# Three unused pieces of storage between the tiles of a two-block transformer kernel

## The chip, the cores and the metric

The kernel runs on 1 core of one Trainium2 chip. The metric is device time in microseconds for one execution; of the kernel before, three runs gave 2788.84, 2790.34 and 2790.70 us, median 2790.34.

## The reference, cut to what matters

256 tokens of width 2048 go through two transformer blocks in float32. Each of their large steps is a product of a [256, 2048] activation with a weight matrix:

```python
x = first_block(x, mem, ...)      # input projection (5136 columns), causal pooling and gated delta rule,
                                  # output projection; cross attention on 256 memory rows; gated
                                  # convolution FFN of width 5632
return second_block(x, c_2, ...)  # modulation vectors from c; projection to NSA and MoBA attention;
                                  # output projection; squared-ReLU FFN of width 8192
# e.g.
h = modulate(rms_norm_2(x, pre_norm_ffn[l]), shift_f, scale_f)
f = jnp.square(jax.nn.relu(h @ w_up[l])) @ w_down[l]
x = x + gate_f[:, None, :] * rms_norm_2(f, post_norm_ffn[l])
```

## The kernel before, in words

**Split products.** Every large product is made of float32r matmuls: an operand is split into a high part and the rest (low part), and high x high, high x low and low x high are summed in PSUM. So each block of a product takes three matmuls, a triple.

**Weights.** `load_to` (L193) brings a unit of 128 x 1024 weights into one of four `w32` buffers by a DMA from SP's queue. `split_to` (L207) makes its high part `wh` on ScalarE (L216) and its low part `wl` on VectorE (L218), three buffers each. The units run in one planned order through the whole program, loaded seven ahead and split two or three ahead.

**Activations.** They lie transposed, features on partitions, in eight tiles A0 to A7 of 8192 bytes per partition, each holding 8 feature blocks of 256 tokens. `act_pair(0)` (L412) is A0, A1 for the high parts and A2, A3 for the low parts; `act_pair(1)` is A4, A5 and A6, A7. The hidden rows of both feed-forward networks and the second block's attention outputs use `hidden` (L1258) with A4 and A6 or A5 and A7, high part first.

**The two loops.** `lin_a` (L285) gives rows of tokens: an activation block of 128 x 128 is stationary and 512 weight columns move (L298, L299, L300). `lin_b` (L304) gives transposed results: a weight block of 128 x 128 is stationary and 256 tokens of an activation block move (L316, L317, L318). In both, the second weight part is read with the activations' high part, and the activations' low part with the high weights:

```python
mm(ps, h, wh[:, k, :], start=kb == 0, stop=False)          # L298, lin_a: stationary first, then moving
mm(ps, h, wl[:, k, :], start=False, stop=False)            # L299
mm(ps, lo, wh[:, k, :], start=False, stop=kb == g.nkb - 1) # L300
mm(ps, wb, h, start=..., stop=False, ...)                  # L316, lin_b
mm(ps, wb, lo, start=False, stop=False, ...)               # L317
mm(ps, wb2, h, start=False, stop=kb == g.nkb - 1, ...)     # L318
```

**Who reads which tiles.** lin_b reads A0 to A3 in the input projection, the queries of the cross attention, gate and up of the first FFN, the second block's projections and its up products; it reads A4 to A7 only for the memory keys (`mk`, L653). lin_a reads A0 to A3 for z, the mixer output and the second block's values; it reads A4 to A7 for the memory values, both attention outputs and the down products of both FFNs.

**Order.** The program records its instructions itself, in the order of the code: after each weight unit `pump` steps the pending tasks (evacuations, norms, attention, the modulation's sums), so that their instructions stand between the matmuls.

**Addresses.** Tiles get their place in the order in which their tags first occur, one after the other, and the weights' buffers follow. By the built program (start in bytes of a partition, modulo 256 and modulo 512):

| tiles | before, mod 256 | after, mod 256 | before, mod 512 | after, mod 512 |
|---|---|---|---|---|
| A0 to A3 | 192 | 128 | 192 | 384 |
| A4, A5 | 0 | 192 | 256 | 448 |
| A6, A7 | 128 | 192 | 384 | 192 |
| wh, wl, w32 (ten buffers) | 192 | 192 | 448 | 448 |
| cst, X, prm, r0 to r3 | 128 | 128 | | |
| most other r and s tiles | 64 | 128 | | |

Blocks within A tiles are 1024 bytes apart, blocks of 128 columns or tokens 512 bytes, so a tile's phase modulo 512 is that of every block that a matmul reads in it.

Of the kernel before, what the change touches and what calls it, by code (L numbers as in the profile page):

```python
# [9 lines left out]
F32 = mybir.dt.float32  # L10
# [5 lines left out]
P = 128  # L16
# [74 lines left out]
class Prog:  # L91
# [21 lines left out]

# [1 line left out]
    def t(self, tag, shape, dt=F32):  # L115
        self.seq += 1
        return self.pool.tile(shape, dt, tag=tag, name=f"{tag}_{self.seq}")

    def col(self, name, n):
# [18 lines left out]

# [1 line left out]
    def start(self, gen, rate=1.0):  # L140
# [21 lines left out]
    def need(self, *tasks):  # L162
        """Steps these tasks to their ends, and the others only where these wait for something."""
        n = 0
        while any(not t["done"] for t in tasks):
            n += 1
            assert n < 10000, "tasks wait for each other"
            self.blocked = False
            for task in tasks:
                self.step(task)  # L170
            if self.blocked:
                for task in list(self.tasks):
                    if task not in tasks and task["rate"] >= 1.0:
                        self.step(task)
# [11 lines left out]

# [1 line left out]
    def plan(self, groups):  # L188
# [42 lines left out]

# [1 line left out]
    def group_start(self):  # L233
# [13 lines left out]
    def lin_small(self, name, n, xh, xl, tag):  # L247
        """[256, 2048] x [2048, n] of few columns in one bank; returns it, with the low parts' products beside."""
        nc = self.nc
# [71 lines left out]

# [1 line left out]
    def c(self, name):  # L323
# [17 lines left out]
    def rms_cols(self, name, parts):  # L341
        """parts [P, 2, n] of partial sums of squares over D -> [P, 2] 1/rms."""
        nc = self.nc
        s = self.col(name + "_s", 2)
        r = self.col(name, 2)
        nc.vector.tensor_reduce(s, parts, axis=AX, op=OP.add)
        self.powm(r, s, 1.0 / D)
        return r

    def row_bcast(self, colv, name, pause=0):  # L350
        """[P, 2] columns -> [P, 256], the same row in every partition."""
        nc = self.nc
        dg = self.t("dd", [P, 2, P])
        for tb, eng in enumerate((nc.gpsimd, nc.vector)):
            eng.tensor_scalar(dg[:, tb], self.c("ident"), colv[:, tb:tb + 1], 1.0, op0=OP.mult, op1=OP.mult)
        yield from self.pause(pause)
        tag, ps = yield from self.get_bank()
        for tb in range(2):
            nc.tensor.matmul(ps[:, tb * P:(tb + 1) * P], self.c("ones"), dg[:, tb], start=True, stop=True)
        row = self.t(name, [P, T])  # L360
        nc.scalar.activation(row, ps[:, :T], AF.Copy)
        self.give(tag)
        return row
# [12 lines left out]
    def lift(self, src, kb0, gcol, dst, nb=4):  # L376
        """Transposes token rows of nb feature blocks, times a column per block, as high and low parts."""
        nc = self.nc
# [17 lines left out]
    def lift_t(self, src, kb0, gcol, dst, nb=4):  # L396
        """The same from rows that come transposed."""
        nc = self.nc
        hi, lo = dst
        for b in range(nb):  # L400
            kb = kb0 + b
            nc.scalar.activation(hi(kb), src[:, b], AF.Copy, scale=gcol(kb))  # L402
            nc.vector.scalar_tensor_tensor(lo(kb), src[:, b], gcol(kb), hi(kb).bitcast(F32),
                                           op0=OP.mult, op1=OP.subtract)
            if b % 2:
                yield
# [5 lines left out]
    def act_pair(self, half):  # L412
        """High and low parts of [2048, 256] in one half of the activations' space."""
        a = [self.t(f"A{4 * half + j}", [P, 8, T], F32R) for j in range(4)]

        def part(o):
            return lambda kb, n=0: a[o + kb // 8][:, kb % 8:kb % 8 + n] if n else a[o + kb // 8][:, kb % 8, :]

        return part(0), part(2)
# [29 lines left out]
    def lift_evac(self, accs, c, parts, gcol, dst):  # L449
        """Adds products to rows, with their squares' sums, and lifts the rows."""  # L450
        nc = self.nc
# [43 lines left out]

# [1 line left out]
    def run(self):  # L497
# [48 lines left out]

# [1 line left out]
        self.consts = {"cst": self.pool.tile([P, _CONST["cst"].shape[1]], F32, name="cst")}  # L548
# [15 lines left out]
        nc.gpsimd.memset(self.mhalf, -0.5)  # L564
        nc.scalar.activation(self.col("first", 8), self.mhalf, AF.Copy)

# [1 line left out]
        self.split_to(1)  # L568
# [38 lines left out]
        A4 = self.t("A4", [P, 2, 4, T])  # L607
        A5 = self.t("A5", [P, 2, 4, T])
        S = [{"k": A4[:, 0], "q": A4[:, 1], "v": A5[:, 0]}, {}]
        self.z = [None, None]  # L610
# [27 lines left out]

# [1 line left out]
        self.y = self.act_pair(0)  # L640
# [15 lines left out]

# [1 line left out]
        yh, yl = self.y  # L658
# [15 lines left out]

# [1 line left out]
        vm = []  # L676
# [11 lines left out]

# [1 line left out]
        oh, ol = self.act_pair(1)  # L690
# [32 lines left out]

# [1 line left out]
    def rr_evac(self, accs, dst, row):  # L725
# [75 lines left out]

# [1 line left out]
    def pool_evac(self, accs, c):  # L803
# [44 lines left out]

# [1 line left out]
    def mem_lift(self, c):  # L850
# [11 lines left out]

# [1 line left out]
    def bc(self, colv):  # L864
# [100 lines left out]
    def dn_batch(self, tb, hs, qT, knT, vb, kbe, kd, o, rq, st):  # L965
# [67 lines left out]
        def even(x, b):  # L1033
            """Columns of the even blocks of b."""
            return x.rearrange("p (n two b) -> p n two b", two=2, b=b)[:, :, 0]
# [56 lines left out]

# [1 line left out]
    def xattn(self, h, qT, kT, v, oh, ol):  # L1094
# [47 lines left out]
    def later_split(self, tag, psv, hi, lo):  # L1142
        """High and low parts of a bank, one step on."""
        def gen():
# [4 lines left out]

# [1 line left out]
    def ada(self, vectors, stage, acct, width):  # L1151
# [44 lines left out]
    def gain_rows(self, gcol, tags):  # L1196
        """[P, 16] columns -> [P, 2048], the same row in every partition."""
        nc = self.nc
# [22 lines left out]

# [1 line left out]
    def gate_evac(self, accs, c):  # L1223
# [67 lines left out]

# [1 line left out]
    def before_mixer2(self):  # L1293
# [29 lines left out]
    def last_evac(self, accs, c):  # L1323
        """Rows after the first block, the two norms' squares, and the rows transposed."""
        nc = self.nc
# [20 lines left out]
    def hold(self, c, take):  # L1346
        """Four transposed feature blocks of the rows in two banks."""
        nc = self.nc
# [11 lines left out]
    def spare_acc(self, pr):  # L1360
        """The accumulators that the group after the next one takes."""
        tag = f"acc{(self.acc_next + 2 + pr) % 4}"
# [4 lines left out]
    def unhold(self, c, G, held, vec=False, prs=(0, 1)):  # L1367
        """Those blocks times columns, in float32."""
        nc = self.nc
# [11 lines left out]
    def modulate(self, c, rr, shift, dst, G=None, held=None):  # L1381
        """Rows' scale and the shift on four blocks, as high and low parts."""
        nc = self.nc
# [135 lines left out]
    def gain_evac(self, accs, dst, c, parts, gr):  # L1519
        """Sums two slabs' products, their rows' squares, and the gains on them."""  # L1520
        nc = self.nc
# [126 lines left out]
    def probs(self, q, k, gate, ptag, stag, nm):  # L1648
        """Causal softmax rows of one head, times a gate, transposed: key block 0 for all 256 queries, then key
        block 1 for the later 128."""  # L1650
        nc = self.nc
# [46 lines left out]
    def nsa_cmp(self, g, qn):  # L1698
        """Gated softmax over the compressed keys, transposed, for four heads; two heads per tile."""
        nc = self.nc  # L1700
# [45 lines left out]
    def nsa_group(self, g, qn, ksw, vsw, oh, ol):  # L1746
        """Four heads; the next head's rows begin while a head's last steps run."""
        nc = self.nc
# [26 lines left out]
    def both(self, gens, apart=0):  # L1775
        """Steps generators side by side, each starting some steps after the one before."""
        out = [None] * len(gens)
# [36 lines left out]

# [1 line left out]
    def relu_evac(self, accs, c, hid):  # L1816
# [11 lines left out]
    def ffn2(self):  # L1828
# [3 lines left out]
        F = [None] * 4  # L1832
        fp = self.parts("f_p")
        hid = {}

# [50 lines left out]
def columns(inputs):  # L1886
    """Small vectors with features on partitions."""
    parts = []
# [43 lines left out]
```

## Time and profile before

| | |
|---|---|
| median of three runs | 2790.34 us (2788.84 to 2790.70) |
| span of the profiled execution | 2786.8 us, first to last instruction |
| TensorE matmul busy | 2736.6 us, 98% |
| TensorE weight load busy | 2514.3 us, 90% |
| VectorE / ScalarE / GpSimd busy | 66% / 47% / 10% |
| HBM traffic | 579.21 MB read, 209 GB/s over the span |

The page is of one execution; its whole time is not listed apart from the span, and the runs' times lie 2 to 4 us above that span. The durations of matmuls overlap: the next one starts while the one before still drains, so the sum of the durations is more than the busy time. The matmul's first named operand is the one that moves, the second is the stationary one.

### The profile page before, as it was taken

The numbers are of one execution on the slowest core, as the hardware profiler recorded it, in microseconds if no ns is written. First come the engines' busy times: TensorE is split into PE (matmuls) and PEld (weight loads), VectorE is DVE, ScalarE is ACT, GpSimd is POOL, SyncE is SP. The second block draws the span as 40 slices with busy tenths as digits, with TensorE's granted clock in tenths as the row PEclk, the third lists the DMA queues.
The fourth block names the chain that finished last, engine by engine and source line by source line (L and its number), as shares of the span: only waits on it lengthen the run. The fifth ranks groups of instructions, "written<-read, shape, count | busy, mean of one in ns | idle before, by whom it ended". The sixth has DMA issues, their size and how long they took to land.

```text
span 2786.8 us, 45609 instructions
## 1 busy us (share of the span) xinstructions
PE 2736.6 (98%) x18322; PEld 2514.3 (90%) x18322; DVE 1849.6 (66%) x2276; ACT 1299.8 (47%) x1894; POOL 290.9 (10%) x249
## 2 busy tenths in 40 slices
PE   8999999999999999999999989999989999999997
PEld 8999998889889999999999789998889988999896
DVE  6665745676787877777777576677575556655555
ACT  6544533544454454444444554444554444444443
POOL 0230201000001020000000031001021000000020
PEclk9999999999999999999999999999999999999999
DMA  8644544787787777777777645443556666656554
GB/s 290 190 129 136 175 129 144 233 292 249 235 265 267 261 256 258 271 260 255 271 257 241 211 149 179 144 144 129 181 167 229 233 219 233 224 184 185 187 181 143
DMA packets 292116, 584.29 MB, mean 210 GB/s; under 512 B 23968, under 2 KB 32288, under 8 KB 291904
## 3 DMA queue, kind: packets, MB, share of 16 engines
q1 hardware_dynamic: 287952, 569.93, 62.5%
q0 software_dynamic: 3232, 10.14, 1.1%
q8 instruction: 143, 2.34, 0.3%
q10 hardware_dynamic: 720, 1.31, 0.1%
q14 instruction: 69, 0.57, 0.1%
HBM read 579.21 MB, written 2.10 MB: 209 GB/s over the span
## 4 chain that ended last, share of the span: by engine, by line
PE 88%; issue 6%; DVE 2%; ACT 1%; POOL 1%; DMA 0%; DVEq 0%; ACTq 0%; POOLq 0%
PE acc L316 16%; PE acc L318 16%; PE acc L317 16%; PE acc L298 11%; PE acc L300 11%; PE acc L299 11%; DVE wl L218 1%; PE m L986 1%; PE m L1039 1%; ACT wh L216 1%; PE m L1046 1%; PE m L1136 0%; PE m L1105 0%; PE m L989 0%; PE m L1694 0%
## 5 line engine op out<-in xcount | busy, mean ns | idle before, releaser
L218 DVE TENSOR_TENSOR wl<-w,wh 128x1024 fp32r<-128x1024 f32 x874 | 1092.0, 1251 | 871.4 <-ACT wh L216 869.1
L216 ACT ACTIVATE wh<-w 128x1024 fp32r<-128x1024 f32 x880 | 928.2, 1058 | 1200.7 <-PE acc L317 652.7
L316 PE MATMUL acc<-A,wh 128*128 128x256 f32 x3968 | 1137.5, 287 | 11.3 <-ACT A L402 7.8
L318 PE MATMUL acc<-A,wl 128*128 128x256 f32 x3968 | 1126.2, 284 | 5.0 <-DVE wl L218 2.7
L317 PE MATMUL acc<-A,wh 128*128 128x256 f32 x3968 | 1125.9, 284 | 0.1
L316 PEld LDWEIGHTS acc<-A,wh 128*128 128x128 f32 x3968 | 761.9, 192 | 13.1 <-ACT A L402 7.8
L318 PEld LDWEIGHTS acc<-A,wl 128*128 128x128 f32 x3968 | 761.6, 192 | 5.6 <-DVE wl L218 2.9
L317 PEld LDWEIGHTS acc<-A,wh 128*128 128x128 f32 x3968 | 762.2, 192 | 2.0 <-DVE A L1400 0.5
L298 PE MATMUL acc<-wh,A 128*128 128x512 f32 x1536 | 612.5, 399 | 2.4 <-ACT wh L216 2.1
L300 PE MATMUL acc<-wh,A 128*128 128x512 f32 x1536 | 608.0, 396 | 0.0
L299 PE MATMUL acc<-wl,A 128*128 128x512 f32 x1536 | 602.9, 393 | 2.0 <-DVE wl L218 2.0
L299 PEld LDWEIGHTS acc<-wl,A 128*128 128x128 f32 x1536 | 288.6, 188 | 69.6 <-DVE wl L218 3.5
L300 PEld LDWEIGHTS acc<-wh,A 128*128 128x128 f32 x1536 | 288.6, 188 | 66.9
L298 PEld LDWEIGHTS acc<-wh,A 128*128 128x128 f32 x1536 | 289.5, 188 | 63.8 <-ACT wh L216 2.6
L1188 DVE SCALAR_TENSOR_TENSOR r<-r,c_silu_c,r 128x1024 f32<-128x1024 f32 x128 | 172.2, 1346 | 0.0
L1822 POOL TENSOR_TENSOR s<-s 128x512 f32<-128x512 f32 x32 | 51.0, 1592 | 574.1 <-ACT s L1821 574.1
L1188 DVE SCALAR_TENSOR_TENSOR s<-s,c_silu_c,s 128x512 f32<-128x512 f32 x128 | 95.8, 749 | 12.0 <-DMA s<-w_ada 10.6
L1243 POOL TENSOR_TENSOR r<-r,rr 128x1024 f32<-128x1024 f32 x11 | 26.8, 2434 | 590.2 <-ACT r L1242 546.4
L1666 ACT ACTIVATE s<-s,c_am 128x128 f32<-128x128 f32 (+1 forms) x48 | 21.5, 448 | 90.3 <-DVE c_am L1664 90.3
L1554 POOL TENSOR_TENSOR r<-r,s 128x512 f32<-128x512 f32 x15 | 25.6, 1706 | 227.8 <-DVE s L1551 227.8
L1239 DVE SCALAR_TENSOR_TENSOR r<-r,prm,r 128x254 f32<-128x254 f32 x88 | 42.3, 481 | 1.6
L374 ACT ACTIVATE dd<-X 128x512 bf16<-128x512 f32 x40 | 25.1, 628 | 23.5 <-DVE X L437 15.8
(368 smaller groups left out, 1636.4 us busy)
## 6 DMA issues: line engine op xcount, KB each, us to landing
w<-w_up SPq DMA_DIRECT2D x216, 512.0 KB, 3.7
w<-w_down SPq DMA_DIRECT2D x216, 512.0 KB, 3.8
w<-w_in SPq DMA_DIRECT2D x152, 512.0 KB, 3.5
r<-w_ada SPq DMA_DIRECT2D x128, 512.0 KB, 5.0
w<-w_gate SPq DMA_DIRECT2D x88, 512.0 KB, 3.9
w<-w_xkv SPq DMA_DIRECT2D x64, 512.0 KB, 3.9
s<-w_ada SPq DMA_DIRECT2D x128, 256.0 KB, 4.8
w<-w_mix_out SPq DMA_DIRECT2D x32, 512.0 KB, 3.6
```

What stands on the lines that cost most here:

```text
L216: nc.scalar.activation(hi[:, :m], src[:, :m], AF.Copy)
L218: eng.tensor_tensor(lo[:, :m], src[:, :m], hi[:, :m].bitcast(F32), op=OP.subtract)
L298: mm(ps, h, wh[:, k, :], start=kb == 0, stop=False)
L299: mm(ps, h, wl[:, k, :], start=False, stop=False)
L300: mm(ps, lo, wh[:, k, :], start=False, stop=kb == g.nkb - 1)
L316: mm(ps, wb, h, start=kb == 0 and b % 2 == 0, stop=False, skip_group_check=True)
L317: mm(ps, wb, lo, start=False, stop=False, skip_group_check=True)
L318: mm(ps, wb2, h, start=False, stop=kb == g.nkb - 1, skip_group_check=True)
L986: return lambda out, h: nc.tensor.matmul(out, lhs(h), rhs(h), start=True, stop=True)
L1188: nc.vector.scalar_tensor_tensor(acc, tiles.pop(n), self.silu_c[:, kb:kb + 1], acc, op0=OP.mult, op1=OP.add)
L1239: nc.vector.scalar_tensor_tensor(cv[:, b, s:], st[:, b, :T - s], w[k], cv[:, b, s:], op0=OP.mult, op1=OP.add)
L1822: nc.gpsimd.tensor_tensor(y, y, y, op=OP.mult)
```

## The change

A method `pad` allots a tile that nothing reads or writes. It is called three times: before A0's first use (48 float32, 192 bytes per partition), after A4 and A5 (128 bytes), and after most other tiles (192 bytes). Tiles that come later in the order move up by that much, so A0 to A5 by 192 bytes, A6, A7 and the scratch by 320 and the weights by 512. Comments and docstrings are taken out as well. The built program has the same instructions in the same order on every engine, with the same waits; only addresses and line numbers differ.

```diff
+    def pad(self, name, n):
+
+        return self.pool.tile([P, n], F32, tag=name, name=name)
...
         nc.scalar.activation(self.col("first", 8), self.mhalf, AF.Copy)
-
-        # ---- first block: input projection ----
+        self.pad("pad0", 48)
+
+
         self.split_to(1)
         xh, xl = self.act_pair(0)
...
         A4 = self.t("A4", [P, 2, 4, T])
         A5 = self.t("A5", [P, 2, 4, T])
+        self.pad("pad1", 32)
         S = [{"k": A4[:, 0], "q": A4[:, 1], "v": A5[:, 0]}, {}]
...
         fp = self.parts("f_p")
+        self.pad("pad2", 48)
         hid = {}
```

## Rows read from the trace of the kernel before

**Rows 1.** The page's head: busy time, share, instructions; granted clock in 40 slices.

```profile
PE 2736.6 (98%) x18322; PEld 2514.3 (90%) x18322; DVE 1849.6 (66%) x2276; ACT 1299.8 (47%) x1894; POOL 290.9 (10%) x249
PEclk9999999999999999999999999999999999999999
```

**Rows 2.** The chain that ended last, by engine.

```profile
PE 88%; issue 6%; DVE 2%; ACT 1%; POOL 1%; DMA 0%; DVEq 0%; ACTq 0%; POOLq 0%
```

**Rows 3.** Waits of PE, longest in total first: us, times, longest.

```profile
PE acc L316 <- ACT A L402: 7.8, 1, 7.8
PE m L1356 <- DVE X L1499: 4.4, 1, 4.4
PE acc L316 <- ACT A L1395: 3.5, 2, 1.7
...
```

**Rows 4.** The page's costliest groups: count, busy us, mean ns, idle before.

```profile
L316 PE MATMUL acc<-A,wh 128*128 128x256 f32 x3968 | 1137.5, 287 | 11.3 <-ACT A L402 7.8
...
L298 PE MATMUL acc<-wh,A 128*128 128x512 f32 x1536 | 612.5, 399 | 2.4 <-ACT wh L216 2.1
```

**Rows 5.** PE in order of time, second FFN, lin_b: start us, duration us.

```profile
2189.83 0.29 PE L316 MATMUL acc<-A,wh 128*128 128x256 f32 x1
...
2198.47 0.28 PE L316 MATMUL acc<-A,wh 128*128 128x256 f32 x1
```

**Rows 6.** Groups by line, PE, 2190 to 2220 us.

```profile
L316 PE MATMUL acc<-A,wh 128*128 128x256 f32 x84 | 23.8, 283 | 0.0
```

**Rows 7.** PE in order of time, memory keys, lin_b.

```profile
321.25 0.28 PE L317 MATMUL acc<-A,wh 128*128 128x256 f32 x1
...
329.38 0.28 PE L317 MATMUL acc<-A,wh 128*128 128x256 f32 x1
```

**Rows 8.** Groups by line, PE, 322 to 329 us.

```profile
L318 PE MATMUL acc<-A,wl 128*128 128x256 f32 x21 | 5.9, 282 | 0.0
L316 PE MATMUL acc<-A,wh 128*128 128x256 f32 x21 | 5.9, 281 | 0.0
L317 PE MATMUL acc<-A,wh 128*128 128x256 f32 x20 | 5.6, 279 | 0.0
```

**Rows 9.** PE in order of time, second FFN, lin_a.

```profile
2504.92 0.39 PE L298 MATMUL acc<-wh,A 128*128 128x512 f32 x1
...
2520.92 0.39 PE L298 MATMUL acc<-wh,A 128*128 128x512 f32 x1
```

**Rows 10.** Groups by line, PE, 2505 to 2540 us.

```profile
L300 PE MATMUL acc<-wh,A 128*128 128x512 f32 x51 | 20.2, 397 | 0.0
L298 PE MATMUL acc<-wh,A 128*128 128x512 f32 x51 | 20.0, 393 | 0.0
L299 PE MATMUL acc<-wl,A 128*128 128x512 f32 x51 | 20.0, 392 | 0.0
```

**Rows 11.** PE in order of time, mixer output, lin_a.

```profile
480.06 0.39 PE L298 MATMUL acc<-wh,A 128*128 128x512 f32 x1
...
495.70 0.39 PE L298 MATMUL acc<-wh,A 128*128 128x512 f32 x1
```

**Rows 12.** Groups by line, PE, 478 to 518 us.

```profile
L298 PE MATMUL acc<-wh,A 128*128 128x512 f32 x59 | 23.1, 391 | 0.0
L300 PE MATMUL acc<-wh,A 128*128 128x512 f32 x59 | 23.0, 389 | 0.0
L299 PE MATMUL acc<-wl,A 128*128 128x512 f32 x59 | 23.0, 389 | 0.0
```

**Rows 13.** Two lines of plain float32 matmuls: duration ns min/median/max, first and last start.

```profile
L1105 PE MATMUL m<-r,r x64: 377/379/380, 648.2 to 762.5; 128*128 128x256 f32 x64
L1136 PE MATMUL m<-s,r x64: 377/379/379, 669.3 to 783.1; 128*128 128x256 f32 x64
```

**Rows 14.** One stretch of the first FFN: busy us of PE, PEld, DVE, ACT, POOL; clock, DMA share, GB/s.

```profile
1010.00:1080.00 70.00, 70.00 (x585) 70.00 (x585) 55.70 (x58) 31.48 (x35) 2.50 (x1) 1.00 0.82 272
```

## The prediction

> **What bounds the kernel now.** I read the page's head first: the matmul engine is busy for 98% of the span and its clock was granted in full in every slice [rows 1]. The chain that ended last is PE for 88% [rows 2]. The waits of that engine are few: the longest kind is one of 7.8 us at the start, then one of 4.4 us, and no later kind is above 3.5 us [rows 3]. So nothing ends late because a transfer, ScalarE or VectorE is late. What sets the time is how fast matmuls follow each other, and nearly all of them are the two linear loops: L316 to L318 (lin_b, activations moving, a weight block stationary) three times 3968, and L298 to L300 (lin_a, weights moving, an activation block stationary) three times 1536 [rows 4].
>
> The change issues no instruction and moves none. It shifts addresses, so the question is whether a matmul's pace depends on where its two operands begin. The kernel before already answers this in part, because its tiles begin at three phases (modulo 256 bytes): A0 to A3 at 192, A4 and A5 at 0, A6 and A7 at 128, and all weights at 192. The same two loops run on each of them. I therefore looked for four stretches in which nothing but one loop runs, and read two things in each: the mean duration of one matmul by line, and the starts of the first and the last matmul, with the number of steps from start to start between them. Durations overlap (283 ns for one, while the next starts 120 ns later), so only differences between durations count; the pace comes from the starts.
>
> - lin_b on A0 to A3, phase 192 against weights at 192: 72 steps from start to start, from 2189.83 to 2198.47 us, 120.0 ns each [rows 5]; L316 takes 283 ns [rows 6].
> - lin_b on A4 to A7 (the memory keys), high parts at 0, low parts at 128: 69 steps from 321.25 to 329.38 us, 117.8 ns each [rows 7]. The lines that read the high parts take 281 and 282 ns, the one that reads the low part (L317) 279 [rows 8].
> - lin_a on A4 to A7 (the second block's last product): 69 steps from 2504.92 to 2520.92 us, 231.9 ns each [rows 9]. High parts at 0: 393 and 392 ns; low parts at 128 (L300): 397 [rows 10].
> - lin_a on A0 to A3 (mixer output), everything at 192: 69 steps from 480.06 to 495.70 us, 226.7 ns each [rows 11]; 391, 389 and 389 ns [rows 12].
>
> All four stretches have the engine full, so these paces are not waits. I read them as two streams that are read at once, the moving operand and the next stationary one, getting in each other's way by an amount that depends on their phases. In lin_b equal phases are the slowest case, in lin_a the fastest.
>
> After the change lin_b on A0 to A3 has activations at 128 and weights at 192, the pairing of L317 in the keys. lin_a on A4 to A7 has both at 192, the pairing of the mixer output. Both large groups move to the best pairing that the trace shows.
>
> **The change part by part.** Counts first. lin_b on A4 to A7 is the memory keys alone: 4 groups x 16 feature blocks x 4 column blocks = 256 triples, 768 matmuls; the rest, 11904 - 768 = 11136, reads A0 to A3. lin_a on A0 to A3 is z (2 groups x 16 blocks x 2 rows = 64 triples), the mixer output (8 x 8 x 2 = 128) and the second block's three value products (3 x 32 = 96): 288 triples, 864 matmuls. The rest, 4608 - 864 = 3744, is on A4 to A7.
>
> 1. lin_b on A0 to A3, 192 to 128. What pace belongs to 128 alone? In the keys the mean duration over the three lines is 280.7 and L317's is 1.7 below it, so 117.8 - 1.7 = 116.1; rows are rounded to 1 ns, and I take 116.5. Gain 3.5 x 11136 = 39.0 us. Bounds: 116.1 gives 43.4 us, the mixed pace 117.8 gives 24.5 us. For nothing at all see the rivals.
> 2. lin_a on A4 to A7, 0 and 128 to 192. By starts 231.9 - 226.7 = 5.2 ns, by durations 394.0 - 389.7 = 4.3 ns; over 3744 matmuls 19.5 and 16.1 us. I take 18.
> 3. The keys, 0 and 128 to 192: 120.0 - 117.8 = 2.2 ns x 768 = 1.7 us lost.
> 4. lin_a on A0 to A3, 192 to 128. No stretch has both parts at 128 there; the nearest row is L300's 397 against 389.7, so 7.3 ns x 864 = 6.3 us lost. If what L299 shows (392) is the truth, 2.0 us; if only a mixture of phases costs, nothing. I take 6.3, since L300 is the line that reads at 128.
> 5. Tiles of rows and scratch also shift, most of them from 64 to 128. Their matmuls are plain float32, and those do not show the phase: L1105 has both operands at 64 in 48 and both at 128 in 16 of its 64 matmuls, L1136 has one at 64 and the other mostly at 128, and both have a median of 379 ns, with 377 and 379 or 380 at the ends [rows 13]. Zero, bounded by 1.8 us either way (18322 - 16512 = 1810 other matmuls [rows 1] and 1 ns each).
> 6. VectorE, ScalarE and the transfers keep their work, and have to follow a faster matmul engine. In the densest stretch transfers took 0.82 of their engines at 272 GB/s [rows 14]; 3% faster is about 0.84, still under full. Waits on evacuations do not shrink; I take 3 us that turn up there, between 0 and 6.
>
> Sum: -39.0 - 18 + 1.7 + 6.3 + 3 = -46 us. The profiled span is 2786.8 us and the whole times of the runs are 2788.84 to 2790.70, 2 to 4 us around it, which stays; I subtract from the median 2790.34: **2744.3 us**. Best ends of the terms: -43.4 - 19.5 + 1.7 + 2.0 = -59, 2731. Worst ends: -24.5 - 16.1 + 1.7 + 6.3 + 6 = -27, 2764.
>
> **Rivals.**
>
> *Mixture.* Not the phase counts but whether high and low parts share one. For it: the keys and the second block's products are the stretches with mixed phases, so the trace can't part the two readings fully. Then lin_b, uniform before and after, stays at 120.0, lin_a on A4 to A7 still gains 18, lin_a on A0 to A3 loses nothing and the keys lose 1.7: 2774 us. Against it: within a mixed stretch L317 and L300, which read at 128, differ from their neighbours in opposite directions, faster in lin_b and slower in lin_a, as a pairing of phases would have it. 0.15.
>
> *Nothing.* The phase is not the cause; the four stretches differ by what else runs. Then the change does not do anything: 2790 us. Against it: stretches 2000 us apart show the split by line. 0.06.
> The Trainium skill speaks for this rival: "TensorE: Matmul & The Clock Gate", "Step-by-step: what each phase is for", says that the engine has two independent SBUF read ports, so that loading the next tile's weights takes nothing from the running matmul. By that no address could matter and the sum would be 0; the 389 against 397 ns by tile [rows 10, 12] disagree with so strong a reading.
>
> *A coarser collision, on the slower side.* Seen modulo 512 the weights begin at 448, and no activation tile did before (192, 256, 384). After the change A4 and A5 begin at 448 too. If two streams that agree in that larger step shut each other out, 2496 matmuls of lin_a (L298, L299) and 512 of the keys pay. Price: the 128 columns of a load stand at the pace of moving ones, 231.9 / 512 x 128 = 58 ns, times 3008 = 174 us, against some 39 us that remain of the gain: about 2925 us. It decides from 15 ns per matmul on. Against it: the largest difference between any two rows is 8 ns. 0.04.
>
> **How the numbers follow.** Forecast 0.75, mixture 0.15, nothing 0.06, collision 0.04. The forecast's own range is 2731 to 2764; to hold 8 in 10 it has to take in the mixture, so 2731 to 2776. A change of 0.2%, 5.6 us, is about what this measurement can tell from none. Forecast and mixture both lie beyond it: faster 0.90, within 0.06, slower 0.04.
>
> **What would show it.** L316 to L318 in the feed-forward stretches at 279 to 280 ns instead of 283, and starts 116 to 117 ns apart, shows step 1; 283 unchanged means mixture. L298 to L300 on A4 to A7 at 389 to 391 instead of 392 to 397 shows step 2, and more than 400 for L298 and L299 the collision. The keys at 283 show step 3, the mixer output near 397 step 4. Busy time of the other engines should stay. I am wrong if these durations move as said and the span does not: then a wait that rows 3 do not show has taken their place.

## The result, and the profile after

The changed kernel takes 2736.1 us, the median of four runs from 2733.63 to 2742.97; the kernel before took 2790.31 in the same series. The ratio is 0.9814 with a 95% interval of 0.9802 to 0.9825. The profiled execution of the changed kernel, the one of 2742.97 us, has a span of 2741.2 us, 45.6 less than before.

The page's groups of the two linear loops show where the time went. First the lines of the kernel before that were not shown yet, then all six of the changed kernel (its line numbers are four higher): count, busy us, mean ns, idle before.

```profile
L318 PE MATMUL acc<-A,wl 128*128 128x256 f32 x3968 | 1126.2, 284 | 5.0 <-DVE wl L218 2.7
L317 PE MATMUL acc<-A,wh 128*128 128x256 f32 x3968 | 1125.9, 284 | 0.1
...
L300 PE MATMUL acc<-wh,A 128*128 128x512 f32 x1536 | 608.0, 396 | 0.0
L299 PE MATMUL acc<-wl,A 128*128 128x512 f32 x1536 | 602.9, 393 | 2.0 <-DVE wl L218 2.0
```

```profile
L320 PE MATMUL acc<-A,wh 128*128 128x256 f32 x3968 | 1125.1, 284 | 11.4 <-ACT A L406 7.7
L322 PE MATMUL acc<-A,wl 128*128 128x256 f32 x3968 | 1113.4, 281 | 6.1 <-POOL wl L222 3.3
L321 PE MATMUL acc<-A,wh 128*128 128x256 f32 x3968 | 1113.6, 281 | 0.4 <-DVE A L407 0.2
...
L302 PE MATMUL acc<-wh,A 128*128 128x512 f32 x1536 | 608.6, 396 | 3.5 <-ACT wh L220 3.2
L303 PE MATMUL acc<-wl,A 128*128 128x512 f32 x1536 | 600.9, 391 | 2.2 <-DVE wl L222 2.2
L304 PE MATMUL acc<-wh,A 128*128 128x512 f32 x1536 | 600.6, 391 | 0.0
```

The counts are the same. With [rows 4], lin_b lost 12.4 + 12.8 + 12.3 = 37.5 us and lin_a 3.9 + 2.0 + 7.4 = 13.3. Since each matmul overlaps the next by nearly the same time, these are nearly differences of pace. The same from the starts of all matmuls, where a step is the time from one start to the next, any wait included, and counts for the matmul that it begins with: lin_b on A0 to A3 1360.7 to 1322.5 us, lin_a on A4 to A7 883.7 to 868.6, lin_a on A0 to A3 202.5 to 204.4, the memory keys 93.2 to 94.1, the steps after all other matmuls 223.9 to 229.0. The sum is -45.4 us, within 0.2 of the change of the span.

What was not expected: lin_b on A0 to A3 has not one pace but two. In the second FFN, groups by line from 2150 to 2190 us and then from 2425 to 2459 us:

```profile
L320 PE MATMUL acc<-A,wh 128*128 128x256 f32 x114 | 32.1, 281 | 0.0
L321 PE MATMUL acc<-A,wh 128*128 128x256 f32 x114 | 32.1, 281 | 0.0
L322 PE MATMUL acc<-A,wl 128*128 128x256 f32 x114 | 32.1, 281 | 0.0
...
L322 PE MATMUL acc<-A,wl 128*128 128x256 f32 x101 | 27.9, 276 | 0.0
L320 PE MATMUL acc<-A,wh 128*128 128x256 f32 x101 | 27.9, 276 | 0.0
L321 PE MATMUL acc<-A,wh 128*128 128x256 f32 x100 | 27.6, 276 | 0.0
```

The same loop, the same tiles, no waits, and 281 ns or 276 where it was 283 [rows 6]. By starts, 69 steps in the first of these stretches and 72 in the second:

```profile
2154.78 0.28 PE L320 MATMUL acc<-A,wh 128*128 128x256 f32 x1
...
2162.91 0.28 PE L320 MATMUL acc<-A,wh 128*128 128x256 f32 x1
...
2429.81 0.28 PE L321 MATMUL acc<-A,wh 128*128 128x256 f32 x1
...
2437.97 0.28 PE L321 MATMUL acc<-A,wh 128*128 128x256 f32 x1
```

That is 117.8 and 113.3 ns, against 120.0 before [rows 5]. A stretch keeps its pace until lin_b ends or small matmuls come between. Cut lin_b on A0 to A3 into 360 pieces of 24 steps with no other matmul inside: 111 run under 115 ns in the changed kernel (called fast below), and none did before.

The other three pairings: lin_a on A4 to A7 (2462 to 2500 us), the keys (319 to 326 us) and the mixer output, lin_a on A0 to A3 (478 to 518 us).

```profile
L304 PE MATMUL acc<-wh,A 128*128 128x512 f32 x57 | 22.2, 389 | 0.0
L302 PE MATMUL acc<-wh,A 128*128 128x512 f32 x56 | 21.8, 389 | 0.0
...
L321 PE MATMUL acc<-A,wh 128*128 128x256 f32 x21 | 5.9, 283 | 0.0
...
L303 PE MATMUL acc<-wl,A 128*128 128x512 f32 x59 | 23.3, 394 | 0.0
L302 PE MATMUL acc<-wh,A 128*128 128x512 f32 x59 | 23.1, 392 | 0.0
L304 PE MATMUL acc<-wh,A 128*128 128x512 f32 x58 | 22.5, 388 | 0.0
```

The first, 389 on all three lines, answers to 392 to 397 [rows 10]; the second, 283 on all three, to 279 to 282 [rows 8]; the third to 389 to 391 [rows 12]. Waits of PE grew. Its busy time on the page went from 2736.6 [rows 1] to 2683.0 us, 53.6 less, while the span lost 45.6, so it idles 8.0 us more. Of these 4.5 us stand after other matmuls, which is most of the 5 us there, 2.5 in lin_b on A0 to A3 and 1.5 in lin_a on A4 to A7. The eleven longest kinds of wait sum to 31.7 us before and 36.9 after. The first two of them after, and the wait for the low weight parts, which was 2.3 before:

```profile
PE acc L320 <- ACT A L406: 7.7, 1, 7.7
PE m L1362 <- DVE X L1505: 4.6, 2, 4.4
...
PE acc L322 <- POOL wl L222: 3.3, 2, 1.9
```

### The profile page after: what moved, and what is told of

It reads as the page before. It is cut to its first block, busy times and chain, and to the rows that moved or that the text cites. A ratio compares the mean times of both kernels' runs of the same rounds, so it can differ in the third digit from the quotient of the medians.

```text
span 2741.2 us, 45609 instructions
## 1 busy us (share of the span) xinstructions
PE 2683.0 (98%) x18322; PEld 2475.7 (90%) x18322; DVE 1848.6 (67%) x2276; ACT 1300.0 (47%) x1894; POOL 289.9 (11%) x249
## 4 chain that ended last, share of the span: by engine, by line
PE 89%; issue 6%; DVE 2%; ACT 1%; POOL 1%; DMA 0%; SPq 0%; DVEq 0%; ACTq 0%; POOLq 0%
PE acc L320 16%; PE acc L321 16%; PE acc L322 16%; PE acc L302 11%; PE acc L303 11%; PE acc L304 11%; PE m L992 1%; DVE wl L222 1%; PE m L1045 1%; PE m L1052 1%; ACT wh L220 1%; PE m L1142 1%; PE m L1111 1%; PE m L995 0%; DMA w<-w_in 0%
## 5 line engine op out<-in xcount | busy, mean ns | idle before, releaser
L320 PE MATMUL acc<-A,wh 128*128 128x256 f32 x3968 | 1125.1, 284 | 11.4 <-ACT A L406 7.7
L322 PE MATMUL acc<-A,wl 128*128 128x256 f32 x3968 | 1113.4, 281 | 6.1 <-POOL wl L222 3.3
L321 PE MATMUL acc<-A,wh 128*128 128x256 f32 x3968 | 1113.6, 281 | 0.4 <-DVE A L407 0.2
L320 PEld LDWEIGHTS acc<-A,wh 128*128 128x128 f32 x3968 | 752.0, 190 | 13.4 <-ACT A L406 7.7
L322 PEld LDWEIGHTS acc<-A,wl 128*128 128x128 f32 x3968 | 757.4, 191 | 6.7 <-POOL wl L222 3.7
L321 PEld LDWEIGHTS acc<-A,wh 128*128 128x128 f32 x3968 | 750.5, 189 | 2.2 <-DVE A L1406 0.6
```

What stands on the lines that cost most here:

```text
L320: mm(ps, wb, h, start=kb == 0 and b % 2 == 0, stop=False, skip_group_check=True)
L321: mm(ps, wb, lo, start=False, stop=False, skip_group_check=True)
L322: mm(ps, wb2, h, start=False, stop=kb == g.nkb - 1, skip_group_check=True)
```

## The experiments

Most kernels differ from the changed kernel by pads alone. Paces from starts are from unbroken stretches of the second FFN, 192 steps of lin_a or 384 of lin_b. "Distance" is where the moving operand begins less where the stationary one begins, modulo 256 bytes unless 512 is named.

**Half of the change: only A4 to A7.**

```diff
-        self.pad("pad0", 48)
...
+        self.pad("pad3", 48)
         A4 = self.t("A4", [P, 2, 4, T])
```

> Half of the change: A0 to A3 stay at 192 as before, A4 to A7 at 192 and weights at 192 as in the changed kernel. Pairing theory (a matmul's pace depends on the distance between the phases of its moving and its stationary operand, modulo 256 bytes): lin_b stays at 120 ns and 283 ns a matmul, lin_a on A4 to A7 at 227 and 389 to 390; the gain is that of the hidden tiles alone, about 15 us, so 2774 to 2777 us. If the two halves depend on each other (for instance through transfers), the time is more than 5 us away from that. If the phase of scratch tiles (which moved too) carried part of the gain, it is below 2770.

2776.77 us, ratio 0.9954 (0.9939 to 0.9969). Groups by line, lin_b from 2180 us, lin_a from 2315 us:

```profile
L320 PE MATMUL acc<-A,wh 128*128 128x256 f32 x98 | 27.7, 283 | 0.0
...
L303 PE MATMUL acc<-wl,A 128*128 128x512 f32 x52 | 20.2, 389 | 0.0
```

The hidden tiles' part is there and lin_b is untouched: lin_a on A4 to A7 868.1 us, as in the changed kernel. Scratch tiles had moved too and carried none of the gain.

**The other half: only A0 to A3.**

```diff
         self.pad("pad0", 48)
...
+        self.pad("pad3", 16)
         A4 = self.t("A4", [P, 2, 4, T])
...
-        self.pad("pad1", 32)
-        self.pad("pad2", 48)
```

> The other half: A0 to A3 at 128, A4 and A5 at 0, A6 and A7 at 128, weights at 192, scratch at 64 as before. Pairing theory: lin_b on A0 to A3 at 116 to 117 ns (281 ns a matmul), lin_a on A4 to A7 unchanged at 392 to 397 ns, lin_a on A0 to A3 some 2 us worse; 38 us gained and 2 lost, 2753 to 2757 us. Mixture theory (only high and low parts of unlike phase matter): no gain, 2790.

2731.39 us (2730.82 to 2732.62), ratio 0.9792 (0.9778 to 0.9807). Both theories missed: this is 57 us, not 36, and no slower than the whole change. lin_b from 2145 us, lin_a from 2275 us:

```profile
L321 PE MATMUL acc<-A,wh 128*128 128x256 f32 x89 | 24.6, 276 | 0.0
...
L304 PE MATMUL acc<-wh,A 128*128 128x512 f32 x51 | 20.2, 397 | 0.0
```

lin_a is as slow as before (881.7 us), but lin_b runs at the fast pace in 290 of 360 pieces and takes 1301.6 us, 21 less than in the changed kernel, although its own phases modulo 256 are the same there. Modulo 512 its distance is 192 here and 448 there; the run of both halves below takes that up. So something beyond the distance modulo 256 decides between 113 and 118. Mixture is refuted all the same: lin_b, uniform, gained.

**Everything 64 bytes lower, distances kept.** `pad0` has 32 instead of 48.

> The changed kernel with everything from A0 on moved down by 64 bytes: A0 to A3 at 64, A4 to A7 and weights at 128, so all distances as in the changed kernel. Pairing theory: time and durations as in the changed kernel, 2733 to 2743 us, lin_b 281 ns, lin_a 389 ns. Rival, the place of each operand by itself counts (for instance where a row of the memory begins): lin_b and lin_a take paces of their own, and at least one of the two moves by 1 ns or more, 4 to 11 us.

2739.28 us (2733.35 to 2740.93), ratio 0.9816 (0.9802 to 0.9831). lin_b from 2150 us and lin_a from 2285 us:

```profile
L322 PE MATMUL acc<-A,wl 128*128 128x256 f32 x100 | 28.1, 281 | 0.0
...
L304 PE MATMUL acc<-wh,A 128*128 128x512 f32 x52 | 20.2, 389 | 0.0
```

lin_b on A0 to A3 sums to 1321.7 us (1322.5 in the changed kernel), lin_a on A4 to A7 to 867.4 (868.6). For this shift the distance counts, not the place of one operand.

**All activations at 64, half a turn from the weights.** Pads of 32, 48, 32 and 16 float32, the second of them ahead of A4.

> All activations at 64, weights at 192: distance 128 for both loops, which no stretch so far had. Pairing theory gives no number of its own; a curve through the distances seen (lin_b 119.8 at 0, 118.3 at 64, 116.1 at 192; lin_a 227 at 0, 229 to 230 at 192, 231 at 64) gives about 117 ns for lin_b (31 us less than before) and 229 to 231 for lin_a on A4 to A7 (3 to 10 us less): 2750 to 2757 us. If the half turn is where the two reads keep out of each other's way altogether, lin_b is at or under 115 ns and the time is under 2735.

2784.03 us, ratio 0.9983 (0.9973 to 0.9992). lin_b 118.7 ns, lin_a 232.3. The half turn is not the best place, and the curve through the other distances was wrong by about 30 us. 19 of them are lin_b's, which gained 12 us and not 31; the curve had taken the mean of two paces, 116.1, for a point. The rest is lin_a's, which lost about 6 us where 3 to 10 had been expected as a gain.

**Both halves, with the distance modulo 512 that the fast run had.** Pads of 32 and 112 float32 after A5 and at the end; the warm-up copy of `mhalf` writes in place.

> Both halves with the distance that the run of the inputs alone had in lin_b: A0 to A3 at 160, weights at 480 modulo 512 (distance 192 modulo 512 as there, 448 in the changed kernel), A4 and A5 at 224 and A6 and A7 at 480, so equal to the weights modulo 256 (distances 256 and 0 for lin_a). All phases themselves are new, only the distances are known. One small warm-up instruction writes in place, so that the pads fit. Theory 512 (the pace depends on the distance modulo 512): lin_b 114 ns (276 ns a matmul), lin_a on A4 to A7 227 ns (389), 15 us under the run of the inputs alone: 2714 to 2720 us. Rival: the inputs alone were faster for another reason (scratch tiles or the place itself); then lin_b is at 116, and the time at 2733 to 2743 us as in the changed kernel.

2734.25 us (2733.09 to 2740.1), ratio 0.9802 (0.9789 to 0.9815). lin_b falls back to the slow pace and theory 512 with it. From 2150 us:

```profile
L320 PE MATMUL acc<-A,wh 128*128 128x256 f32 x100 | 28.1, 281 | 0.0
```

Fast pieces are there, 128 of 360, in part in other stretches than in the changed kernel. This is what led to the theory of two modes, that is, of two paces at the same distance, each of which holds itself once a stretch is in it.

**Three more distances.** Only pads; the distances of lin_b are 64, 160 and 224.

> lin_b's last unseen distance in steps of 64: A0 to A3 at 192, weights at 128 modulo 512, distance 64. A4, A5 are at 384 (lin_a 256: 227 ns expected), A6, A7 at 0 (lin_a 128: 232 expected). So far lin_b showed 119.8 at 0 and 256, 118.5 at 128, 114.0 at 192, 118.3 at 320, 118.6 at 384, 116.0 at 448. Theory 512 gives no value; a period of 256 with a small correction would give about 118 as at 320, and 2770 to 2776 us.

> A step of 32 bytes: A0 to A3 at 192, weights at 32 modulo 512, distance 160, between 118.5 (128) and 114.0 (192). If the memory is told apart in steps of 64 bytes or more, lin_b is at one of the two neighbours; if it is a smooth curve, near 116; if 160 is the best, under 114. lin_a: A4, A5 at distance 288, A6, A7 at 128; not equal, so near 229 to 232.

> A step of 32 bytes to the other side: A0 to A3 at 192, weights at 480 modulo 512, distance 224, between 114.0 (192) and 119.8 (256). Steps of 64: one of the two neighbours; smooth: near 117; a best value near the equal phase: under 114. lin_a: A4, A5 at 224, A6, A7 at 96; near 229 to 235.

2764.42, 2773.54 and 2781.03 us; lin_b holds 117.8, 117.3 and 118.3 ns in the second FFN. The first time is 6 us under what was expected. Steps of 32 bytes do make a difference: 117.3 at 160 is under the slow paces at 128 and 192, 118.3 at 224 lies between those at 192 and 0. Neither neighbour of 192 shows a piece under 115 ns; at distance 64, 34 of 360 pieces do. More than one pace is not a matter of 192 alone: at 160 about a third of the pieces hold 118.7 and some 120.0, and at 128 some hold 120.0. With lin_a at 231.2, 231.1 and 233.3 none of these layouts comes near the changed kernel.

**One small matmul at the entry, of seven widths.** lin_b gets an argument, `kick`, the width of one extra matmul ahead of its first; it is used in the second FFN:

```diff
+            if kick and kb0 == 0:
+                mm(accs[0][:, :kick], wh[:, 0, :P], xh(0)[:, :kick], start=True, stop=True, skip_group_check=True)
...
-                           ready=ready if c == 0 else None)
+                           ready=ready if c == 0 else None, kick=0 if c % 2 else 16 * c)
```

> The changed kernel with one more matmul at the start of every second up product of the second FFN (the first lin_b after a lin_a), of 32, 64, 96, 128, 160, 192 and 224 columns in turn; the next matmul overwrites its result, so nothing of the computation changes. Theory of two modes: at the distance of the changed kernel lin_b has two paces that hold themselves, 113.3 and 117.8 ns a matmul, and which one a stretch falls into is decided at its entry; without the kick these entries fell into 117.8 six times of seven. Then some widths give 113.3 for the whole stretch of two products (0.6 us less per product) and others 117.8, and nothing between. Rival: the pace is a matter of what else runs in that stretch (transfers, the modulation's sums); then the kick changes nothing after the first few matmuls, and the stretches keep the paces they had: 117.8 but in the one from 2415 us on.

One execution, 2733.14 us. L322 to L324 are lin_b's three lines here. Widths 32, 64, 96, 128, 192 and 224, from 2065, 2145, 2235, 2322, 2500 and 2590 us, one line of three alike each:

```profile
L323 PE MATMUL acc<-A,wh 128*128 128x256 f32 x86 | 24.2, 281 | 0.0
...
L323 PE MATMUL acc<-A,wh 128*128 128x256 f32 x89 | 24.6, 276 | 0.0
...
L324 PE MATMUL acc<-A,wl 128*128 128x256 f32 x89 | 24.6, 276 | 0.0
...
L324 PE MATMUL acc<-A,wl 128*128 128x256 f32 x86 | 24.2, 281 | 0.0
...
L323 PE MATMUL acc<-A,wh 128*128 128x256 f32 x89 | 24.6, 276 | 0.0
...
L322 PE MATMUL acc<-A,wh 128*128 128x256 f32 x86 | 24.2, 281 | 0.0
```

64, 96 and 192 columns give the fast pace for the rest of the stretch, 128 and 224 the slow one, nothing lies between, and the 32 columns, which came in the middle of a fast stretch, ended it. (The stretch with 160 is broken by other matmuls. Without the kick it began slow and was fast behind them, so five of the seven stretches were slow throughout, not six. And 4.5 ns are 0.86 us for a product of 192 matmuls, not 0.6.) The tiles, the phases and the other engines' work are as in the changed kernel, so the entry decides. Each width was tried once here, and 128 and 224 gave what these stretches did without a kick; only the 64 columns are tried again, below.

**The kernel before without the weights' transfers and splits.**

```diff
+            if u >= 4 and m == 1024:
+                hi, lo = self.kept
...
+            if self.loaded >= 4 and nk * g.n == 1024:
+                self.loaded += 1
+                continue
```

> The kernel before in its own layout, but only the first four weight units are loaded and split; all later products read the fourth unit's parts, so the products are wrong and ScalarE's high parts, VectorE's low parts and the weights' transfers are gone. Theory that the matmul engine's own two reads (moving operand and next stationary operand) get in each other's way: paces stay at 120.0 ns for lin_b and 231 ns for lin_a on A4 to A7, 2740 to 2790 us. Rival, that its reads collide with the other engines' or the transfers' accesses to the same addresses: lin_b goes to 116 or less, lin_a to 227 or less, and the time by 100 us.

One execution, 2764.03 us. lin_b from 2160 us, lin_a from 2298 us, then busy us of PE, PEld, DVE, ACT, POOL, the clock, DMA share and GB/s of the first of these stretches, and of one with the same work in the kernel before:

```profile
L332 PE MATMUL acc<-A,wl 128*128 128x256 f32 x98 | 27.8, 283 | 0.0
...
L314 PE MATMUL acc<-wh,A 128*128 128x512 f32 x51 | 20.2, 397 | 0.0
L312 PE MATMUL acc<-wh,A 128*128 128x512 f32 x51 | 20.0, 393 | 0.0
...
2160.00:2195.00 35.00, 35.00 (x294) 35.00 (x293) 4.47 (x4) 2.35 (x4) 2.10 (x2) 1.00 0.10 31
...
2190.00:2225.00 35.00, 35.00 (x294) 35.00 (x294) 19.57 (x18) 14.98 (x17) 3.19 (x2) 1.00 0.69 229
```

The transfers fell to 31 GB/s and VectorE and ScalarE to 4.47 and 2.35 us of 35; the paces are those of before, 120.0 and 231.8. Of the 25 us that the run is shorter, 14.7 are idle time of the matmul engine before matmuls (35.7 to 21.0 us). The effect of the phases is not one of other engines or transfers. What is left is the matmul engine with its own two reads. That these are what collides is argued from this and from the shifted kernel; no run here takes one of the two reads away.

**A version that uses it.** The changed kernel, with the 64-column matmul wherever lin_b follows lin_a in the two FFNs, ten times; and, beside it, at the start of every lin_b (there the argument is 64 for all 62 products). The edit of the first:

```diff
+                           ready=ready if c == 0 else None, kick=64 if s > 1 and j == 0 else 0)
...
+                           ready=ready if c == 0 else None, kick=64 if c % 2 == 0 and c > 2 else 0)
```

> The changed kernel with one 64-column matmul at the start of each stretch of lin_b that follows lin_a in the two feed-forward networks, 10 stretches in all. Theory of two modes, with the entry deciding: the six stretches of the second network run at 113.3 ns as in the survey's stretch with 64 columns (five of them were at 117.8: 5 x 1.7 us), and of the first network's four the parts that were at 117.8 do so until small matmuls come between (up to 8 us); 2718 to 2728 us, under the run of the inputs alone (2731). Rival, that the survey's paces were chance: no more than half of the stretches at 113.3, 2730 to 2742 us.

> The same 64-column matmul at the start of every lin_b product, those too that follow another lin_b. Theory of two modes: what the kick does depends on the state that it meets; after lin_a as in the run before this one, and in a running stretch it may end the fast pace as the 32 columns in the survey did. If it is neutral there, 2715 to 2725 us; if it ends the fast pace, the second half of each stretch is at 117.8, and the time 2728 to 2738 us.

The first takes 2723.39 us (2721.22 to 2725.27), ratio 0.9766 (0.9752 to 0.9781), below all others here. lin_b from 2140 us:

```profile
L324 PE MATMUL acc<-A,wl 128*128 128x256 f32 x104 | 28.7, 276 | 0.0
```

285 of 360 pieces are fast, lin_b on A0 to A3 takes 1303.9 us and lin_a on A4 to A7 has 867.4: both gains at once. All ten stretches with a kick go over to 113.3 within the first 24 steps. The second takes 2744.91 us, ratio 0.9846 (0.9829 to 0.9862), 7 us above what was expected. The kick ends the fast pace where it meets one, and lin_b on A0 to A3 is back at 1321.0 us, 17 more than with ten kicks. That is no more than in the profiled execution of the changed kernel, 1322.5; why the median is above that kernel's too is not shown. The first and the second product of one stretch, from 2153 and 2175 us:

```profile
L322 PE MATMUL acc<-A,wh 128*128 128x256 f32 x51 | 14.1, 276 | 0.0
...
L323 PE MATMUL acc<-A,wh 128*128 128x256 f32 x49 | 13.8, 281 | 0.0
```

## Why the prediction was right, and where a step was not

- **What bounds the kernel.** Right: the span fell by what the two loops lost, less 5 us at the other matmuls. That pace follows the distance of the two operands' phases stands after the shifted kernel, and "nothing" is ruled out. One reading was off: a 9 on the page is 90% or more, and the clock was not granted in full all the time. In the kernel before it was 0.50, the lower of its two levels, from 2030 to 2035 us; in the 5 us ahead of that the matmul engine was busy for 0.59. The mean over the span is 0.993 in both kernels, so the clock is no part of the change.
- **Step 1, lin_b on A0 to A3: -39.0 forecast, -38.2 measured.** The size is right by luck, its ground is not. I took 116.5 ns as the pace that belongs to 128 against 192. There are two, 117.8 and 113.3, with 281 and 276 ns and not the 279 to 280 that I gave as the sign, and the mean over this execution happens to be near my number. What failed is carrying L317's 279 from a stretch of mixed phases to one where all lines read at 128. The keys could not show the two paces: their mixed phases held 117.8. With the other half left out the same step is worth 59 us.
- **Step 2, lin_a on A4 to A7: -18 forecast, -15.1 measured.** The pace went from 231.9 to 226.7 as read; over 3744 matmuls that would be 19.5. On average over their steps only the second FFN's products gained nearly that, 5.1 ns a matmul; the other products on these tiles, with more other matmuls between, gained 4.1 to 4.4. Without idle time the step is 16.7, near my sum over durations (16.1), and 1.5 us more of idle time came with it.
- **Step 3, the keys: +1.7 forecast, +0.9 measured.** As stated, 283 ns on all three lines.
- **Step 4, lin_a on A0 to A3: +6.3 forecast, +1.9 measured.** Mis-sized. I gave L300's 397 to the phase 128 alone. With both parts at 128 the lines take 392, 394 and 388, so the 397 belongs to a low part at 128 between high parts at 0. The lower end, 2.0, was the size.
- **Step 5, plain float32 matmuls: nothing.** Right: without idle time the steps after all other matmuls are 211.5 us before and 212.1 after; the other 4.5 of their 5.1 us are waits.
- **Step 6, +3 of waits, 0 to 6.** Mis-sized: idle time of the matmul engine grew by 8.0 us. 4.5 of it is at the other matmuls, nearly all the rest is inside the figures of steps 1 and 2. The stretch that I called the densest was not: transfers had 0.86 of their engines from 557 to 627 us before. They were not full there after either, 0.87 from 545 to 617 us.
- **Sum.** -46 forecast, worked out from the profiled execution, and -45.6 measured there. That they agree so closely is luck too, since the errors of steps 2, 4 and 6, of 2 to 4 us each, cancel. The median fell by 54, to 8 us under the forecast, because the profiled execution is the slowest of the four; they spread over 9 us, against 2 before. Two paces, of which an execution can take either behind a break, would spread runs so, but only one execution of the kernel was profiled, so this stays a supposition.
- **The rivals.** Mixture fell with step 1. The coarser collision did not come: A4 and A5 at the weights' own phase modulo 512 run at the same 389 ns as A6 and A7, which are 256 away. The Trainium skill ("TensorE: Matmul & The Clock Gate", "Step-by-step: what each phase is for") has loading the next weights take nothing from the running matmul. The run without the splits speaks against that for these matmuls, with 393 against 397 ns by tile while hardly anything else touched the memory; which read waits for which is not shown.
- **What I did not see.** The two halves are not independent. Equal phases for the hidden tiles win 15 us in lin_a, and lin_b, entered from that even pace, then falls into its slow mode. By starts, eleven stretches of lin_b follow directly on lin_a on A4 to A7. With equal phases there all eleven begin at 117.8 ns, in the changed kernel, the shifted one and the one with both halves alike. With the inputs alone, where that lin_a has its old phases, all eleven begin with a first piece of 114.0 to 114.4 and go on at 113.3. That is where the 21 us of the gain on the inputs went: 12.5 in the first FFN, 8.6 in the second. A kick at the entry takes most of it back. What it is in the lin_a before that decides is not shown.

## What to carry to other kernels

In a kernel that is bound by back-to-back float32r matmuls, compare mean durations of the same loop between stretches that use different buffers: a difference of a few ns by buffer, with no waits, points to where the buffers begin, and a few unused bytes can be worth 2%. Try the halves of such a change apart, and look at every stretch by itself: a mean over a run can hide two paces. Where a loop can hold more than one pace, what comes right before it is part of its cost.

## What the runs showed of the hardware that was not expected

- Distance of moving and stationary operand modulo 256 and lin_b's held pace in the second FFN (128 x 128 stationary, 256 moving columns, float32r): 0 gives 120.0 ns, 64 117.8 (113.3 in 34 of 360 pieces of the whole run), 128 118.7, 160 117.3, 192 117.8 or 113.3, 224 118.3. lin_a (512 moving columns): equal phases 226.7, half a turn 232.3.
- At distance 192 two paces hold themselves for hundreds of matmuls. One matmul of 64, 96 or 192 columns between lin_a and lin_b led into the fast one; 128 and 224 did not (one stretch for each width, and ten more for 64).
- Taking away nearly all work of VectorE, ScalarE and the transfers changed no pace of the two loops in the second FFN by more than 0.1 ns.
- Two lines of plain float32 matmuls showed no such dependence (377 to 380 ns at equal and unequal phases [rows 13]).
